# When GpSimd issues its steps of weight sums in a one-core decoder layer

## The chip, the core and the metric

The kernel runs on one core of a Trainium2 chip. The core has TensorE (matrix products, into PSUM), VectorE, ScalarE, GpSimd and SyncE, each with a queue of its own that it works through in order, and sixteen DMA engines that serve the queues of DMAs that SyncE, ScalarE and GpSimd issue. The metric is the device time of one launch in microseconds; lower is better. A time stands for the median of several runs.

## The reference

One layer of a hybrid decoder on 2048 tokens of width 1024, all in float32:

```python
h = rmsnorm(x, mix_norm_g)
q, k, v, g, u = split(h @ w_in)                     # 4 x 512 columns and 512 for the pooling
y_ret  = silu(g) * head_rmsnorm(retention(q, k, v, positions), ret_gn_g)
y_pool = pool_mixer(u, pool_w, pool_scale)
x = x + concat([y_ret, y_pool]) @ w_out
x = x + cross_attn(rmsnorm(x, xa_norm_g), mem_n, wq, wkv, wo)     # 4 heads, 256 memory tokens
a = rmsnorm(x, ffn_norm_g) @ w_up                   # 2 * 2816 columns
c = causal depthwise convolution of width 3 along the tokens, plus a bias
x = x + (silu(c_gate) * c_val) @ w_down
return rmsnorm(x, final_norm_g)
```

Retention and the rotary embedding use `positions`; the cross-attention is a softmax over the 256 memory tokens.

## The kernel before

**Precision and products.** A float32 product is made of three passes of TensorE in a reduced format: each operand is split into a high and a low part (`split`, lines 230 to 237: ScalarE makes the high part, VectorE the low one), and `passes` (lines 239 to 243) issues high x high, high x low, low x high. A `unit` (line 287) multiplies 128 output columns by 1024 tokens: two weight halves times two token halves, so four quarters of twelve passes.

**Stages.** The tokens are worked on in two blocks of 1024 (`for b in range(NB)`, from line 1547 on). Ahead of them stands `folded_weights`, which multiplies weights of the attention and of the pooling with one another; part of it (`wqT`, `wo`, `wout_p`) is spread over the projections of the first block. A block then has:

- its input projections: values, four heads (gate, q, k: three units each, with the retention of the head before spread over them) and four pooling groups, 16 units in all;
- its output projection: 8 units, with the residual `xT` loaded into temporaries `T` ahead of time, the result stored to `Xd` by a DMA that ScalarE issues (L816);
- its attention (`attention`, line 824): for two pairs of heads, eight tiles of tokens each, 16 iterations. The folded weights `Md` are loaded and split ahead (`load_m`, L837); an iteration makes scores on TensorE, softmax on VectorE and ScalarE (L875 to L884), and two iterations later the transposes L852. The norm's statistics (L317 on TensorE, then small steps on VectorE) are taken at the first iteration;
- beside the first block's attention, the rotary tables of the second block (`rope_tables`, line 548), which load `pos` (L555) into a temporary and run on VectorE;
- the attention's output units with `VWd`, and in the first block the loads of the second block's `xT`.

After both blocks comes the gated MLP, which uses a seven-product scheme (Strassen's kind) for its matrix products. It needs sums of weight blocks, and these are what GpSimd makes.

**The steps of weight sums.** `weight_sums` (lines 907 to 941) has 34 jobs: 22 for `w_up` and 12 for `w_dn`. A job has four stages, eight DMAs from DRAM to DRAM: four plain copies (L921), then two, one and one DMAs that add to what is there (L918). A step starts one job and advances those under way by one stage, so that most steps issue eight DMAs of 192 or 256 KB, and there are 37 steps. A step is paced by a tiny ScalarE copy (L936), which `keep_in_program_order` pins behind the ScalarE instruction traced just ahead of it; a GpSimd copy (L937) waits for it, and the step's DMAs are queued behind that on GpSimd. The sums are needed when the MLP starts.

**When a step is taken.** `under[0]` is the generator. Every call of `next(under[0])` is a tick: the first takes a step, and then `spacing[0]` ticks pass until the next:

```python
for _ in range(spacing[0]):
    yield
```

Ticks come from the quarters of `unit` (L301; in the first block's projections, while `slow[0]` is true, from every other quarter) and from the iterations of `attention` (L889; in the first block from i = 5 on). The spacing is 4 at first, 8 in the first block's output projection, 2 in the attentions, 4 afterwards. During the attention's output units the generator is set aside (`paused`).

**The order of work.** The engines' queues are put in order ahead of the run by a scheduler that plans with its own model of times (only the MLP's end is ordered by hand). Each queue is then worked off as planned. SyncE issues nearly all loads, in order, each when its buffer is free: five places `R` for weights, ten temporaries `T`.

Of the kernel before, what the change touches and what calls it, by code (L numbers as in the profile page):

```python
# [119 lines left out]
def trunk(ctx, tc, xT, memT, pos, w_qkgu, w_v, wkv, wqT, wo, wout_r, wout_p, poolT, w_up, w_dn, vecs, consts, outT):  # L120
# [17 lines left out]
    def new_z(dtype):  # L138
        return Arena(cp.tile([P, 8 * T + 4 * EDGE], dtype, tag="Z", name=nm("Z")), 0, 8, T)
# [58 lines left out]
    def mmps():  # L198
        return mmp.tile([P, SUB], F32, tag="mm", name=nm("mm"))
# [6 lines left out]
    def aux():  # L206
        if both[0] and next(turns_) % 3 == 2:
            return single()
        return auxp.tile([P, SUB], F32, tag="aux", name=nm("aux"))

    def small(n=4):
        t = smp.tile([P, 8], F32, tag="sm", name=nm("sm"))
        return t[:, :n]

    def tt(eng, out, a, b, op):
        return eng.tensor_tensor(out=out, in0=a, in1=b, op=op)  # L216

    def ts(eng, out, a, s1, op0, s2=None, op1=None):
        if op1 is None:
            eng.tensor_scalar(out=out, in0=a, scalar1=s1, scalar2=None, op0=op0)  # L220
        else:
            eng.tensor_scalar(out=out, in0=a, scalar1=s1, scalar2=s2, op0=op0, op1=op1)
# [7 lines left out]
    def split(src, hi, lo, g=None):  # L230

        if g is None:
            act.activation(hi, src, AF.Copy)  # L233
            tt(dve, lo, src, hi.bitcast(F32), ALU.subtract)
        else:
            act.activation(hi, src, AF.Identity, scale=g)
            stt(lo, src, g, hi.bitcast(F32), ALU.mult, ALU.subtract)

    def passes(ps, lhs, rhs, start, stop, more=False):
        (lh, ll), (rh, rl) = lhs, rhs  # L240
        pe.matmul(ps, lh, rh, start=start, stop=False, skip_group_check=more)  # L241
        pe.matmul(ps, lh, rl, start=False, stop=False, skip_group_check=more)  # L242
        latest[0] = pe.matmul(ps, ll, rh, start=False, stop=stop, skip_group_check=more)  # L243

    def new_raw():
        r = raws.take()
        r.free()
        return r.f
# [6 lines left out]
    def pairs(raw):  # L255

        out = []
        for h in range(2):
            r = raw[h] if isinstance(raw, list) else raw[:, h * SUB : (h + 1) * SUB]
            pr = new_pair()  # L260
            split(r, pr[:, 0], pr[:, 1])
            out.append(pr)
        return out
# [14 lines left out]
    quarter, slow, spacing = [0], [True], [4]  # L278
# [8 lines left out]
    def unit(raw, rhs, evac, order=range(4)):  # L287


        hs = raw if isinstance(raw, list) else pairs(raw)  # L290
        ps = [mmps() for _ in range(NS)]
        for h in range(2):
            for s in range(NS):
                for j, kk in enumerate(order):
                    k = 4 * h + kk
                    w = [hs[h][:, i, kk * P : (kk + 1) * P] for i in range(2)]
                    passes(ps[s], w, rhs(k, s), h + j == 0, h == 1 and j == 3)
                next(behind[0], None)
                quarter[0] += 1
                if not slow[0] or quarter[0] % 2:  # L300
                    next(under[0], None)  # L301
                if h == 1:
                    evac(s, ps[s])
# [520 lines left out]
    def attention(sums, beside, pace):  # L824


        scl, nscl = (smp.tile([P, 8], F32, tag="scl", name=nm("scl"), bufs=2) for _ in range(2))
        room = B.take(2 * KT)
        third = [Region(B, room.first + KT * i, KT) for i in range(2)] + [new_z(F32R).take(KT)]
        prob = [third[1], third[0]]  # L830

        def load_m(hp):

            out = mw[hp]
            for kp in range(KT // 2):
                raw = new_raw()
                fetched[0] = sp.dma_start(raw.rearrange("p (k n) -> p k n", k=2), Md[hp, 2 * kp : 2 * kp + 2].rearrange("k p n -> p k n"))  # L837
                if hp == 0 and kp == 0:

                    out += [(pr[:, 0], pr[:, 1]) for pr in pairs(raw)]  # L840
                    yield
                    continue
                for i in range(2):
                    u = third[2 * hp].r[:, (2 * kp + i) * T : (2 * kp + i + 1) * T]
                    split(raw[:, i * SUB : (i + 1) * SUB], u[:, :SUB], u[:, SUB:])
                    out.append((u[:, :SUB], u[:, SUB:]))
                yield

        def turn(pt, t, e):
            tp = aux()  # L850
            for j in range(4):
                pe.transpose(tp[:, j * P : (j + 1) * P], e.f[:, j * P : (j + 1) * P], ident)  # L852
            pt4 = pt.r.rearrange("p (i k t) -> p i k t", i=2, t=T)[:, :, :, t * P : (t + 1) * P]
            turned.append(act.activation(pt4[:, 0], tp.rearrange("p (k t) -> p k t", k=4), AF.Copy))
            tt(dve, pt4[:, 1], tp.rearrange("p (k t) -> p k t", k=4), pt4[:, 0].bitcast(F32), ALU.subtract)
            e.free()

        turned.clear()
        mw = [[], []]
        for _ in load_m(0):  # L860
            pass
        more_m = load_m(1)
        late = []
        for i in range(2 * KT):
            hp, t = divmod(i, KT)
            ps = mmps()
            for k in range(KT):
                x2 = [X[:, 2 * k + j, t * P : (t + 1) * P] for j in range(2)]
                passes(ps, x2, mw[hp][k], k == 0, k == KT - 1)
            if i == 0:  # L870
                rn, _, _ = norm_tables(sums, wide=False)
                ts(dve, scl, rn, 1.0 / 16.0, ALU.mult)
                ts(dve, nscl, rn, -1.0 / 16.0, ALU.mult)
            mx, sm = small(2), small(2)
            dve.reduce_max(out=mx, in_=ps.rearrange("p (h m) -> p h m", h=2), axis=AX.X)  # L875
            ts(dve, mx, mx, nscl[:, t : t + 1], ALU.mult)
            e = TT.take()
            for j in range(2):
                act.activation(e.f[:, j * NMEM : (j + 1) * NMEM], ps[:, j * NMEM : (j + 1) * NMEM], AF.Exp,
                               bias=mx[:, j : j + 1], scale=scl[:, t : t + 1], accum_out=sm[:, j : j + 1])  # L880
            dve.reciprocal(sm, sm)
            for j in range(2):
                ej = e.f[:, j * NMEM : (j + 1) * NMEM]
                ts(dve, ej, ej, sm[:, j : j + 1], ALU.mult)  # L884
            if len(late) == 2:
                turn(*late.pop(0))
            late.append((prob[hp], t, e))
            if pace > 1 or i > 4:
                next(under[0], None)  # L889
            if i < KT - 2:  # L890
                next(more_m, None)
            else:
                for _ in range(pace):
                    next(beside, None)

        def end():
            for one in late:
                yield turn(*one)

        return prob, end()  # L900
# [142 lines left out]
    class Up(Member):  # L1043
# [15 lines left out]
        def evac(self, i, ps):  # L1059
            if i == 0:  # L1060
                self.gate = self.place()
            elif i == 1:
                self.val = self.place()
            which, q, how = ((0, 0, 0), (1, 1, 0), (0, 1, 0), (0, 0, 1), (1, 1, 1), (0, 1, 1), (1, 0, 0))[i]
            d = body(self.val if which else self.gate)[:, q * SUB : (q + 1) * SUB]
            if how:
                tt(dve, d, d, ps, ALU.add)
            else:
                act.activation(d, ps, AF.Copy)
            if i > 4:  # L1070
                pending.extend(self.conv(i - 5))
# [396 lines left out]
    def norm_tables(s_acc, wide=True, late=False):  # L1468

        rn = rows_norm(s_acc)  # L1470
        rb, last = [], None
        if wide:
            rb = [TT.take() for _ in range(NS)]
            last = spread(rn, [r.f[:, :SUB] for r in rb], late=late)
        return rn, rb, last
# [71 lines left out]
    for b in range(NB):  # L1547
# [29 lines left out]
        for r in rb:  # L1577
            r.free()
        mix += [pooled[g] for g in range(4)]
        slow[0], spacing[0] = False, (8, 4)[b]  # L1580

        xs = [TT.take() for _ in range(NS)]
        ahead = fetch_x(b, 0)
# [15 lines left out]
        beside = tables() if b + 1 < NB else first_tiles(own)  # L1599
        spacing[0] = (2, 2)[b]  # L1600
        prob, behind[0] = attention(xs, beside, b + 1)
        spacing[0] = 4
        for _ in beside:
            pass
        under, paused = [iter(())], under
# [14 lines left out]
        for n in range(KT):  # L1620
# [3 lines left out]
            def rhs(k, s):  # L1624
                at = (k % 4) * T + s * SUB
                return tuple(prob[k // 4].r[:, i * 4 * T + at : i * 4 * T + at + SUB] for i in range(2))
# [159 lines left out]
```

## Time and profile before

| | |
|---|---|
| median of 3 runs | 2476.74 us (2476.66 to 2477.2) |
| the profiled execution's own time | 2477.48 us |
| its span, first to last instruction | 2475.5 us |
| TensorE busy | 2434.9 us (98%) |
| VectorE, ScalarE busy | 1707.9 us (69%), 1223.2 us (49%) |
| GpSimd busy | 272.1 us (11%) |
| mean granted TensorE clock | 0.994 |
| bytes that the steps' queue (q0) moved | 69.22 MB, 12.4% of the sixteen DMA engines' span |

The page is read from the busy shares to the chain of work that ended last and from there to the waits: idle time of an engine matters only where that engine sets the end. Below, a row of the timeline has the start and the length in us, then engine, line, operation, what it writes and reads and, in brackets, how long its engine stood idle ahead of it and what ended that. A row of the waits has who waited for whom, the total in us, the number of times, the longest. A row of the windows has its stretch and length, then busy time and count for TensorE, its weight loads, VectorE, ScalarE and GpSimd, then the granted clock, the DMA engines' busy share and GB/s. A row of a DMA queue has its packets, MB, and the time that its packets took as a share of all engines; a row of DMA issues has the size of each and the median time from issue to landing.

### The profile page before, as it was taken

What the parts mean: (1) busy time and instruction counts of PE and PEld (TensorE: products, weight loads), DVE (VectorE), ACT (ScalarE), POOL (GpSimd) and SP (SyncE); (2) the same over time, 40 slices, a digit from 0 to 9 for tenths busy, and PEclk for the clock granted to TensorE, in tenths of its full rate; (3) what the DMA queues carried; (4) which work ended last, traced back from release to release, by engine and by line L of the source; (5) the groups of instructions that cost most, each with busy time, mean ns of one, the idle gap of its engine ahead of it and who ended that gap; (6) DMA issues with size and microseconds to landing.
All of it is one profiled execution on the core that took longest, in us unless ns stands there. A gap on an engine that the chain in (4) does not pass through costs nothing.

```text
span 2475.5 us, 33058 instructions
## 1 busy us (share of the span) xinstructions
PE 2434.9 (98%) x11390; PEld 2036.2 (82%) x11390; DVE 1707.9 (69%) x2913; ACT 1223.2 (49%) x2207; POOL 272.1 (11%) x413
## 2 busy tenths in 40 slices
PE   6999999999999999999999999999999999999997
PEld 6888888888888888888888888888888888888886
DVE  8645666565635675574678776897667688867876
ACT  6333423353421223434655565665555677666663
POOL 1001022131113430000000010020000000000000
PEclk8999999999999999999999999999999999999998
DMA  8145677767636767356468665665546468768951
GB/s 287 65 136 159 203 177 196 222 141 246 183 101 154 189 165 205 111 196 246 145 200 283 204 189 158 220 215 174 160 155 217 135 225 301 247 189 276 348 173 68
DMA packets 248216, 474.27 MB, mean 192 GB/s; under 512 B 26864, under 2 KB 54128, under 8 KB 248048
## 3 DMA queue, kind: packets, MB, share of 16 engines
q1 hardware_dynamic: 193328, 374.62, 46.4%
q0 software_dynamic: 30208, 69.22, 12.4%
q10 hardware_dynamic: 24512, 28.32, 3.3%
q8 instruction: 89, 1.46, 0.2%
q14 instruction: 79, 0.65, 0.1%
HBM read 370.87 MB, written 170.39 MB: 219 GB/s over the span
## 4 chain that ended last, share of the span: by engine, by line
PE 96%; DVE 1%; DMA 1%; ACT 1%; issue 0%; POOLq 0%; POOL 0%; SPq 0%; DVEq 0%; ACTq 0%
PE mm L241 30%; PE mm L243 30%; PE mm L242 30%; PE aux L764 1%; PE aux L751 1%; PE aux L852 1%; PE aux L740 1%; PE aux L766 1%; PE aux L317 1%; DMA R<-wo 1%; PE aux L241 1%; PE aux L243 1%; PE aux L242 1%; DVE Z L216 0%; DVE Q L216 0%
## 5 line engine op out<-in xcount | busy, mean ns | idle before, releaser
L241 PE MATMUL mm<-G,Q 128*128 128x512 f32 (+1 forms) x1888 | 727.0, 386 | 17.1 <-ACT Q L233 10.9
L243 PE MATMUL mm<-G,Q 128*128 128x512 f32 (+1 forms) x1888 | 725.7, 385 | 5.8 <-DVE Q L216 5.6
L242 PE MATMUL mm<-G,Q 128*128 128x512 f32 (+1 forms) x1888 | 724.8, 384 | 0.0
L241 PE MATMUL mm<-G 128*128 128x512 f32 (+1 forms) x1380 | 529.0, 385 | 3.1 <-ACT T L474 3.0
L242 PE MATMUL mm<-G 128*128 128x512 f32 (+1 forms) x1380 | 530.8, 385 | 0.0
L243 PE MATMUL mm<-G 128*128 128x512 f32 (+1 forms) x1380 | 528.8, 385 | 0.0
L241 PEld LDWEIGHTS mm<-G,Q 128*128 128x128 f32 x1888 | 358.1, 190 | 86.0 <-ACT Q L233 11.5
L243 PEld LDWEIGHTS mm<-G,Q 128*128 128x128 f32 x1888 | 357.6, 190 | 75.4 <-DVE Q L216 7.1
L242 PEld LDWEIGHTS mm<-G,Q 128*128 128x128 f32 x1888 | 358.1, 190 | 67.9 <-DVE G L216 0.4
L241 PEld LDWEIGHTS mm<-G 128*128 128x128 f32 x1380 | 260.0, 188 | 54.8 <-ACT T L474 3.2
L242 PEld LDWEIGHTS mm<-G 128*128 128x128 f32 x1380 | 260.0, 188 | 51.5
L243 PEld LDWEIGHTS mm<-G 128*128 128x128 f32 x1380 | 259.9, 188 | 51.4
L1023 ACT ACTIVATE G<-R 128x512 fp32r<-128x512 f32 (+1 forms) x272 | 167.0, 615 | 251.2 <-PE mm L242 244.2
L216 DVE TENSOR_TENSOR Z<-Z,mm 128x512 f32<-128x512 f32 x284 | 193.8, 683 | 102.2 <-PE mm L243 102.0
L216 DVE TENSOR_TENSOR Q<-R,Q 128x512 fp32r<-128x512 f32 x235 | 162.6, 695 | 147.2 <-ACT Q L233 133.0
L225 DVE SCALAR_TENSOR_TENSOR Z<-Z,vecs 128x1024 f32<-128x1024 f32 x176 | 224.8, 1281 | 49.9 <-ACT Z L1086 46.4
L216 DVE TENSOR_TENSOR G<-R,G 128x512 fp32r<-128x512 f32 (+1 forms) x268 | 178.4, 675 | 107.7 <-ACT G L1023 75.0
L233 ACT ACTIVATE Q<-R 128x512 fp32r<-128x512 f32 x150 | 93.7, 629 | 259.9 <-PE mm L242 220.0
L1023 ACT ACTIVATE Q<-R 128x512 fp32r<-128x512 f32 (+1 forms) x204 | 125.5, 615 | 96.0 <-PE mm L242 80.4
L216 DVE TENSOR_TENSOR G<-T,G 128x512 fp32r<-128x512 f32 (+1 forms) x201 | 133.2, 677 | 44.2 <-ACT G L972 29.1
L216 DVE TENSOR_TENSOR T<-T 128x512 f32<-128x512 f32 (+3 forms) x218 | 149.5, 690 | 19.3 <-ACT T L357 11.2
L1086 ACT ACTIVATE Z<-Z,vecs 128x1024 f32<-128x1024 f32 x88 | 109.2, 1242 | 34.0 <-DVE Z L216 33.1
(216 smaller groups left out, 2623.2 us busy)
## 6 DMA issues: line engine op xcount, KB each, us to landing
R<-Ud SPq DMA_DIRECT2D x176, 256.0 KB, 2.8
T<-Gd SPq DMA_DIRECT2D x168, 256.0 KB, 4.4
Ud<-w_up POOLq DMA_DIRECT2D x132, 256.0 KB, 8.9
R<-w_up SPq DMA_DIRECT2D x132, 256.0 KB, 3.3
Gd<-Z SPq DMA_DIRECT2D x110, 256.0 KB, 2.8
R<-w_qkgu SPq DMA_DIRECT2D x32, 512.0 KB, 4.4
R<-Dd SPq DMA_DIRECT2D x64, 256.0 KB, 4.2
Gd<-T SPq DMA_DIRECT2D x56, 256.0 KB, 3.5
```

Source lines behind the costliest of these rows:

```text
L216: return eng.tensor_tensor(out=out, in0=a, in1=b, op=op)
L225: dve.scalar_tensor_tensor(out=out, in0=a, scalar=s, in1=b, op0=op0, op1=op1)
L233: act.activation(hi, src, AF.Copy)
L241: pe.matmul(ps, lh, rh, start=start, stop=False, skip_group_check=more)
L242: pe.matmul(ps, lh, rl, start=False, stop=False, skip_group_check=more)
L243: latest[0] = pe.matmul(ps, ll, rh, start=False, stop=stop, skip_group_check=more)
L317: pe.matmul(ps[:, t : t + 1], ap, one, start=True, stop=more is None)
L740: pe.matmul(col(sc, c), self.ch(k, c), self.ch(q, c), start=True, stop=True)
L751: pe.matmul(col(self.kv, c), col(self.kn.f, c), self.ch(v, c, h * T), start=True, stop=True)
L764: pe.matmul(col(y, c), col(self.pr.f, c), self.ch(v, c, h * T), start=True, stop=self.cur[c] is None)
L1023: act.activation(p2[:, 0, :w], self.raw[i].f[:, :w], AF.Copy)
L1086: act.activation(self.c[g].f, a[:, 2:], AF.Identity, bias=cb[:, f : f + 1], scale=cw[2][:, f : f + 1])
```

## The change

Four values change. In the first block's projections no tick comes any more (before: every other quarter). In its attention the ticks start at i = 2, not at i = 5. The spacing in its output projection is 4 instead of 8, and in the second block's projections 3 instead of 4.

```diff
@@ -297,7 +297,7 @@
                     passes(ps[s], w, rhs(k, s), h + j == 0, h == 1 and j == 3)
                 next(behind[0], None)
                 quarter[0] += 1
-                if not slow[0] or quarter[0] % 2:
+                if not slow[0]:
                     next(under[0], None)
                 if h == 1:
                     evac(s, ps[s])
@@ -885,7 +885,7 @@
             if len(late) == 2:
                 turn(*late.pop(0))
             late.append((prob[hp], t, e))
-            if pace > 1 or i > 4:
+            if pace > 1 or i > 1:
                 next(under[0], None)
             if i < KT - 2:
                 next(more_m, None)
@@ -1577,7 +1577,7 @@
         for r in rb:
             r.free()
         mix += [pooled[g] for g in range(4)]
-        slow[0], spacing[0] = False, (8, 4)[b]
+        slow[0], spacing[0] = False, (4, 4)[b]
 
         xs = [TT.take() for _ in range(NS)]
         ahead = fetch_x(b, 0)
@@ -1599,7 +1599,7 @@
         beside = tables() if b + 1 < NB else first_tiles(own)
         spacing[0] = (2, 2)[b]
         prob, behind[0] = attention(xs, beside, b + 1)
-        spacing[0] = 4
+        spacing[0] = 3
         for _ in beside:
             pass
         under, paused = [iter(())], under
```

## The prediction

> **What bounds the kernel now.** I read the page first: the span, the busy shares, the chain of work that ended last.
>
> ```profile
> span 2475.5 us, 33058 instructions
> PE 2434.9 (98%) x11390; PEld 2036.2 (82%) x11390; DVE 1707.9 (69%) x2913; ACT 1223.2 (49%) x2207; POOL 272.1 (11%) x413
> PE 96%; DVE 1%; DMA 1%; ACT 1%; issue 0%; POOLq 0%; POOL 0%; SPq 0%; DVEq 0%; ACTq 0%
> ```
>
> TensorE is the bound. GpSimd's steps are not on the chain, so moving them gains only where their transfers now make TensorE wait, and costs only where they will make it wait. So I next read the waits of TensorE from 60 to 960 us, the stretch in which all steps run.
>
> ```profile
> PE mm L241 <- ACT T L474: 3.0, 1, 3.0
> PE mm L241 <- ACT G L233: 0.9, 1, 0.9
> PE mm L241 <- ACT T L492: 0.3, 1, 0.3
> ```
>
> That is everything: 4.2 us. The one of 3.0 us lies in the first block's projections, among the steps that the change takes away. The timeline around it, and the issues of two loads of `wo` (us from issue to landing stand last; the first load was issued at 191.1 us, the second at 205.2 us):
>
> ```profile
> 200.87 0.19 POOL L937 COPY halo<-halo 128x2 f32<-128x2 f32 x1 [55.39 <-ACT halo L936]
> 203.02 3.03 POOL L921 DMA_DIRECT2D Ud<-w_up  x4
> 212.59 1.15 ACT L233 ACTIVATE G<-R 128x512 fp32r<-128x512 f32 x2 [8.14 <-DMA R<-wo]
> 220.79 1.15 ACT L233 ACTIVATE G<-R 128x512 fp32r<-128x512 f32 x2 [5.81 <-DMA R<-wo]
> 222.37 0.82 ACT L474 ACTIVATE T<-mm,vecs 128x256 f32<-128x256 f32 x2
> 223.24 0.58 PE L241 MATMUL mm<-G 128*128 128x256 f32 x1 [2.99 <-ACT T L474]
> ...
> R<-wo SPq DMA_DIRECT2D x1, 512.0 KB, 3.7
> R<-wo SPq DMA_DIRECT2D x1, 512.0 KB, 7.4
> ```
>
> The third step starts at 200.87 us and GpSimd is still issuing its DMAs at 206. The `wo` load of 205.2 us goes out into them and takes 7.4 us, not 3.7. ScalarE stands still for it (8.14 us), issues the next split, stands still again for the next load (5.81 us), and only then empties the PSUM bank (L474) that TensorE needs. The stall has a second price, in the granted clock (the number ahead of the last two of a row; TensorE's busy time is the second):
>
> ```profile
> 220.30:223.20 2.90, 0.00 (x0) 0.00 (x0) 0.95 (x3) 2.41 (x6) 0.00 (x0) 0.97 0.00 0
> 223.20:227.20 4.00, 3.96 (x21) 3.96 (x22) 2.99 (x5) 3.50 (x9) 0.00 (x0) 0.59 0.41 136
> 930.00:936.00 6.00, 5.14 (x21) 3.60 (x20) 3.90 (x6) 2.32 (x5) 2.67 (x4) 1.00 1.06 288
> ```
>
> After 2.99 us of idleness the clock is 0.59 for 4.0 us: 0.41 x 4.0 = **1.6 us** more. The 0.9 us stall at 931 us left it at 1.00.
>
> **The change part by part.** 34 jobs with four stages each make 37 steps. By the counts of calls (a step, then as many empty calls as the spacing says) they lie before: 8 in the first block's projections, 4 in its output projection, 6 in its attention, 16 in the second block's projections, 3 in its output projection; after: 0, 8, 7, 22, 0.
>
> *Each step's own instructions.* These move and are not added: one ScalarE copy, one GpSimd copy, eight DMAs.
>
> ```profile
> L936 ACT ACTIVATE halo<-consts x37: 187/189/221, 80.0 to 937.0; 128x2 f32<-128x2 f32 x37
> 385.04 0.72 POOL L937 COPY halo<-halo 128x2 f32<-128x2 f32 x1 [19.17 <-ACT halo L936]
> 387.86 3.38 POOL L921 DMA_DIRECT2D Ud<-w_up  x4
> 450.38 0.55 POOL L937 COPY halo<-halo 128x2 f32<-128x2 f32 x1 [15.76 <-ACT halo L936]
> 514.16 0.46 POOL L937 COPY halo<-halo 128x2 f32<-128x2 f32 x1 [57.71 <-ACT halo L936]
> ```
>
> ScalarE: 4 + 1 + 6 more copies of 0.19 us in three stages, under its idle time (49% busy). GpSimd: a step holds it from 385.04 to 391.2 us, and in these stages it has nothing behind the steps that anything waits for. Both I cost at nothing. The cost is in the DMA engines.
>
> *First block's projections.* Without the third step the load of 205.2 us lands 7.4 - 3.7 = 3.7 us earlier, all behind it on ScalarE moves up by as much, and L474 ends before TensorE is ready (it waits 2.99 us). Gain 2.99 + 1.6 = **4.6 us**. What is late next: the 0.3 us at L492, far from any step; I leave it. Bounds of the gain: 0 (if that load stays slow) to 5.8 (with the 0.9 and 0.3 us waits gone too).
>
> *First output projection, 8 steps for 4.* Shares of the sixteen DMA engines by queue from 385 to 483 us (q0 carries the steps, q1 SyncE's loads, q10 ScalarE's stores):
>
> ```profile
> q0 software_dynamic: 3584, 8.39, 37.8%
> q1 hardware_dynamic: 5575, 11.09, 35.1%
> q10 hardware_dynamic: 2173, 3.96, 11.0%
> ```
>
> Four steps took 0.378 x 98 = 37 us of all engines, 9.3 us each; loads and stores took 45 us. Eight steps take 74: together 119 us in a stretch of 98. So the steps run late by about 20 us and are still moving data from 483 to 500 us, where before there were none between 465 and 514. Inside the output projection I see no stall: TensorE never waits from 380 to 660 us though four steps already lie there, and `xT`, the weights and `Md` are fetched at least a unit (11 us) ahead. Its end and the start of attention are another matter.
>
> *Start of the first attention.* The timeline (ScalarE twice, VectorE twice, TensorE):
>
> ```profile
> 481.06 0.63 ACT L233 ACTIVATE Z<-R 128x512 fp32r<-128x512 f32 x1 [0.88 <-DMA R<-Md]
> 481.07 0.33 ACTq L816 DMA_DIRECT2D Xd<-T  x1
> ...
> 489.35 0.49 DVE L220 TENSOR_SCALAR T<-T,consts 128x512 f32<-128x512 int32 x1 [5.13 <-DMA T<-pos]
> 496.77 0.62 DVE L220 TENSOR_SCALAR T<-T,sm 128x256 f32<-128x256 f32 x2
> ...
> 498.78 0.60 PE L852 MATMUL aux<-consts,T 128*128 128x128 f32 x4
> ```
>
> A serial chain: ScalarE waits for the third `Md` load and then issues the store of `Xd`; its landing (485.8 us) frees the temporary into which SyncE loads the positions; VectorE waits for those (5.13 us) with the first multiplication of the rotary table, and the statistics of the norm are queued behind it; so are the first softmax and its last scaling, which ends at 497.39. TensorE's transposes L852 start at 498.78. **The whole chain has 1.4 us of slack.** Its transfers now, in order Md, Xd, pos, with q1 in 469 to 489 us; then like loads beside steps (674 to 693 us: q1, `w_qkgu`, `rope_d`; at 408 to 412 us: Xd):
>
> ```profile
> q1 hardware_dynamic: 1696, 4.46, 64.1%
> R<-Md SPq DMA_DIRECT2D x3, 512.0 KB, 4.8
> Xd<-T ACTq DMA_DIRECT2D x1, 256.0 KB, 4.7
> T<-pos SPq DMA_DIRECT2D x2, 128.0 KB, 2.9
> ...
> q1 hardware_dynamic: 1009, 3.15, 42.1%
> R<-w_qkgu SPq DMA_DIRECT2D x5, 512.0 KB, 9.5
> T<-rope_d SPq DMA_DIRECT2D x2, 256.0 KB, 8.8
> Xd<-T ACTq DMA_DIRECT2D x4, 256.0 KB, 8.7
> ```
>
> No row shows this chain beside steps, so I bound it. Lowest: no delay. Highest: each link as slow as its like, 4.7 + 4.0 + 5.9 = 14.6 us. Between: q1 moves 4.46 MB here in 20 us; beside steps it moved 3.15 MB in 19 us, 0.166 MB/us, at which 4.46 MB take 26.9 us, and the positions come last. I take that, **6.9 us**, since it is the row of the same queue with as many large loads in a line. TensorE then waits 6.9 - 1.4 = 5.5 us, and 1.6 us for the clock as at 223 us: **7.1 us**.
>
> [...]
>
> *Rest of attention, second block's projections.* 7 steps for 6 start with i = 2, every 11 us: 65 us of engine time where little else moves; the end is no later than before. In the second block, 22 steps of 9.3 us, 205 us in some 260, beside one 512 KB load of `w_qkgu` per unit, fetched units ahead; and by the pinning to ScalarE's preceding instruction (L936), those of ticks 4 to 10 gather behind the first pool evacuation, away from the `rope_d` loads. Cost 0. The second output projection loses three steps: it has one wait of 0.9 us, on a split that no DMA feeds; gain 0.
>
> Sum: -4.6 + 7.1 = +2.5 us. The profiled execution took 2477.48 us (span 2475.5), the median of the runs is 2476.74; 2476.74 + 2.5 = **2479.2 us**.
>
> **The rivals.**
> (a) Attention's start doesn't stall: the steps are done by then, or VectorE's order puts the norm's statistics ahead of the positions. For it: the order is made anew for each program. Against: in this one VectorE stood 5.13 us before the positions, so the planner already takes that load for earlier than it is. Time: 2476.74 - 4.6 = 2472.1; with every wait gone, 2470.9.
> (b) Slower: the three links add up in full. For it: they are serial by wait, not only by bandwidth, and q10's stores compete too. 14.6 - 1.4 + 1.6 - 4.6 = +10.2: 2486.9. A delay above 4.4 us loses more than the projections gain; above 9.4 us the loss passes 0.2%.
> (c) The `wo` stall stays (another order on ScalarE, another load in the way) and the attention's comes on top: +7.1, 2483.8. Against: only that step's DMAs lay across that load.
>
> **How the numbers follow.** Chances: forecast 0.45, (a) 0.30, (b) 0.17, (c) 0.08. About 0.2% (5 us) is what a measurement of this kernel can tell from no change: below 2471.8 is faster, above 2481.7 slower. Faster takes a third of (a): 0.10. Slower takes (b), (c) and a sixth of the forecast: 0.32. The rest, 0.58, is within. Range 2471.6 to 2486.0: it cuts the ends of (a) and (b). The forecast's own: 2476 to 2483.
>
> **What would show it.** Right: no wait at L474 near 220 us and a clock of 1.00 from 213 to 240; q0 busy from 385 to about 590 without a pause; a wait of TensorE of some 5 us before L852 near 494 to 500 us, VectorE waiting for `T<-pos` about 12 us, and a clock below 1 after it; no step behind the second block's projections. Wrong: a wait for `wo` in the projections, no wait at L852, or new waits of TensorE in the output projection or in the second block (loads late that I called covered).

## The result and the profile after

The changed kernel takes **2485.94 us** (median of six runs, 2485.05 to 2486.32) against 2477.55 for the kernel before on the same chip (six runs, 2476.66 to 2478.64). The ratio is 1.0033 with a 95% interval of 1.0020 to 1.0046: **8.4 us slower**. The profiled execution has a span of 2484.1 us. Of the eleven runs of one kernel below (spacing 3 alone) one took 4285.6 us at a granted clock of 0.57; its median is that of the other ten. From the page of after, in the order in which the page of before was read:

```profile
span 2484.1 us, 33049 instructions
...
PE 2438.0 (98%) x11390; PEld 2037.7 (82%) x11390; DVE 1708.1 (69%) x2913; ACT 1223.8 (49%) x2207; POOL 269.4 (11%) x413
...
PE 92%; DMA 3%; DVE 3%; ACT 1%; issue 1%; POOLq 0%; SPq 0%; POOL 0%; ACTq 0%; DVEq 0%
```

The work is the same: TensorE has 11390 matrix instructions in both. Its share of the chain fell from 96% to 92%, and VectorE's and the DMAs' rose to 3% each, so the loss shows as waits; TensorE's own busy time grew by 3.1 us, which fits the slower clock behind them. The next view is again that of TensorE's waits (who waited for whom, total, number, longest), for after from 60 to 1250 us (behind that the waits are the same four in both kernels):

```profile
PE aux L317 <- DVE T L216: 3.4, 1, 3.4
PE mm L243 <- DVE Q L216: 3.0, 1, 3.0
PE aux L751 <- ACT T L746: 1.0, 1, 1.0
PE mm L241 <- ACT G L233: 0.9, 1, 0.9
PE mm L241 <- ACT T L474: 0.8, 1, 0.8
PE mm L242 <- DVE Q L216: 0.7, 1, 0.7
PE aux L852 <- DVE T L220: 0.6, 1, 0.6
```

The wait at L474 shrank from 3.0 to 0.8 us. Two of 3 us are new, and VectorE is named in both. To place them I follow the same instructions through both kernels. The view of one source line has the count, the shortest, median and longest duration in ns, and the first and last start; the landmark is the first start. Before, then after:

```profile
L317 PE MATMUL aux<-consts,Z x16: 206/250/352, 62.0 to 63.9; 128*128 128x1 f32 x16
...
L740 PE MATMUL aux<-Z x8: 275/275/275, 348.1 to 348.9; 128*128 128x128 f32 x8
...
L317 PE MATMUL aux<-consts,T x16: 164/250/250, 482.8 to 487.6; 128*128 128x1 f32 x16
...
L317 PE MATMUL aux<-consts,T x32: 164/250/250, 666.0 to 678.6; 128*128 128x1 f32 x32
```

```profile
L317 PE MATMUL aux<-consts,Z x16: 167/250/250, 61.2 to 62.8; 128*128 128x1 f32 x16
...
L740 PE MATMUL aux<-Z x8: 275/275/275, 343.8 to 344.5; 128*128 128x128 f32 x8
...
L317 PE MATMUL aux<-consts,T x16: 164/250/271, 483.6 to 493.2; 128*128 128x1 f32 x16
...
L317 PE MATMUL aux<-consts,T x32: 164/250/250, 672.8 to 685.3; 128*128 128x1 f32 x32
```

The differences are -0.8, -4.3, +0.8 and +6.8 us. So the first block's projections gained 3.5 us, the output projection lost 5.1, the first attention with its output units lost 6.0, and 1.8 us came after that. Of these, 1.1 us lie in the last part of the run: from the end of the wait at L319 to that of the wait at L1269 before takes 5.05 us and after 6.15, with the clock at half from 2.3 us ahead of that end in before and from 5.8 us ahead in after (2462.2 of 2464.5 and 2467.3 of 2473.0 us). No edit reaches that place, and the traces of the other kernels have 5.04 to 6.40 us there, so I take it for the scatter of single executions. So, in part at least, are the 0.8 us by which this one was ahead at its start (granted clock from 28 to 63 us: 0.80 in before, 0.85 in after). The remaining 0.7 us I leave open.

**The first loss, at 408 us.** The DMA queues and issues of the stretch from 392.5 to 402 us, first before, then after:

```profile
q0 software_dynamic: 471, 1.31, 46.6%
...
T<-xT SPq DMA_DIRECT2D x5, 256.0 KB, 3.3
```

```profile
q0 software_dynamic: 519, 1.31, 60.0%
...
T<-xT SPq DMA_DIRECT2D x6, 256.0 KB, 9.1
```

The residual's loads go out into two steps in a row (GpSimd's copies at 391.57 and 399.96 us) and take 9.1 us instead of 3.3. What follows in after, in order of time:

```profile
405.79 0.69 DVE L216 TENSOR_TENSOR T<-T,mm 128x512 f32<-128x512 f32 x1 [1.74 <-DMA T<-xT]
...
409.70 0.69 DVE L216 TENSOR_TENSOR T<-T,mm 128x512 f32<-128x512 f32 x1 [3.22 <-DMA T<-xT]
410.30 0.68 DVE L216 TENSOR_TENSOR Q<-R,Q 128x512 fp32r<-128x512 f32 x1
...
411.04 0.50 PE L243 MATMUL mm<-G,Q 128*128 128x512 f32 x1 [2.96 <-DVE Q L216]
```

VectorE stands for the residual. TensorE does not need the residual; it needs the low part of the next weights (Q), which is queued behind it. Before, the same three additions ran without a wait for a load:

```profile
407.76 1.97 DVE L216 TENSOR_TENSOR T<-T,mm 128x512 f32<-128x512 f32 x3 [2.90 <-PE mm L243]
```

**The second loss, at the attention's start.** Step eight is late: GpSimd takes it up at 462.62 us, must wait with its adding DMAs for those of earlier stages, and issues its last DMA after 472.88. The three last `Md` loads take 9.3 us (before: 4.8). They also go out 4.2 us later than in before (477.17 against 472.97): the `Md` load ahead of them, issued just before step eight, landed at 471.31 us instead of 467.12, and the splits that set the places in `R` free, its own and those behind it on ScalarE, moved by as much.

```profile
462.62 0.20 POOL L937 COPY halo<-halo 128x2 f32<-128x2 f32 x1
...
465.96 0.85 POOL L918 DMA_DIRECT2D Ud<-Ud  x1 [3.13 <-DMA Ud<-Ud]
...
472.88 2.41 POOL L921 DMA_DIRECT2D Ud<-w_up  x4
...
486.18 1.15 ACT L233 ACTIVATE Z<-R 128x512 fp32r<-128x512 f32 x2 [5.49 <-DMA R<-Md]
...
489.00 0.63 ACT L233 ACTIVATE Z<-R 128x512 fp32r<-128x512 f32 x1 [0.17 <-DMA R<-Md]
...
490.57 0.61 ACT L357 ACTIVATE T<-T 128x512 f32<-128x512 f32 x1
...
491.67 0.68 DVE L216 TENSOR_TENSOR T<-T 128x512 f32<-128x512 f32 x1
492.40 1.05 PE L317 MATMUL aux<-consts,T 128*128 128x1 f32 x8 [3.35 <-DVE T L216]
...
498.01 0.49 DVE L220 TENSOR_SCALAR T<-T,consts 128x512 f32<-128x512 int32 x1 [5.66 <-DMA T<-pos]
```

ScalarE splits `Md` as it lands; the squares of the last residual (L357) are queued behind, and the statistics L317 need them. The positions come after that, at 498 us, and cost 0.6 us more at L852. Both losses have a second price in the clock (windows; the number ahead of the last two is the granted clock):

```profile
408.00:411.00 3.00, 0.08 (x1) 0.00 (x0) 1.30 (x3) 0.58 (x2) 0.00 (x0) 1.00 1.09 285
411.00:414.00 3.00, 2.96 (x10) 2.35 (x11) 3.00 (x6) 2.24 (x5) 0.00 (x0) 0.74 1.05 385
414.00:417.00 3.00, 3.00 (x11) 2.41 (x10) 1.80 (x3) 0.00 (x0) 0.00 (x0) 0.69 1.03 378
...
494.50:498.50 4.00, 4.00 (x12) 3.09 (x12) 0.49 (x2) 0.00 (x0) 0.00 (x0) 0.59 0.45 149
```

Worked out from these windows, that is 0.26 x 3 + 0.31 x 3 = 1.7 us after the first and 0.41 x 4 = 1.6 us after the second. With the waits that makes 3.0 + 1.7 + 0.7 (L242, at 478 us) = 5.4 us against the 5.1 of the landmarks, and 3.4 + 0.6 + 1.6 = 5.6 against 6.0.

### The profile page after: what moved, and what is told of

The parts are those of the page before. It is cut to its first block, busy times and chain, and to the rows that moved or that the text cites. A ratio compares the mean times of both kernels' runs of the same rounds, so it can differ in the third digit from the quotient of the medians.

```text
span 2484.1 us, 33049 instructions
## 1 busy us (share of the span) xinstructions
PE 2438.0 (98%) x11390; PEld 2037.7 (82%) x11390; DVE 1708.1 (69%) x2913; ACT 1223.8 (49%) x2207; POOL 269.4 (11%) x413
## 4 chain that ended last, share of the span: by engine, by line
PE 92%; DMA 3%; DVE 3%; ACT 1%; issue 1%; POOLq 0%; SPq 0%; POOL 0%; ACTq 0%; DVEq 0%
PE mm L243 29%; PE mm L241 29%; PE mm L242 29%; DVE T L216 1%; DMA T<-Xd 1%; DVE Z L216 1%; PE aux L751 1%; PE aux L764 1%; PE aux L740 1%; PE aux L766 1%; PE aux L317 1%; PE aux L243 1%; PE aux L241 1%; PE aux L242 1%; DMA T<-xT 0%
## 5 line engine op out<-in xcount | busy, mean ns | idle before, releaser
L241 PE MATMUL mm<-G,Q 128*128 128x512 f32 (+1 forms) x1888 | 727.5, 386 | 16.1 <-ACT Q L233 10.2
L243 PE MATMUL mm<-G,Q 128*128 128x512 f32 (+1 forms) x1888 | 726.4, 386 | 8.8 <-DVE Q L216 8.7
L242 PE MATMUL mm<-G,Q 128*128 128x512 f32 (+1 forms) x1888 | 725.4, 385 | 0.0
L242 PE MATMUL mm<-G 128*128 128x512 f32 (+1 forms) x1380 | 530.2, 385 | 0.0
L241 PE MATMUL mm<-G 128*128 128x512 f32 (+1 forms) x1380 | 528.4, 385 | 0.8 <-ACT T L474 0.8
L243 PE MATMUL mm<-G 128*128 128x512 f32 (+1 forms) x1380 | 528.2, 385 | 0.0
L241 PEld LDWEIGHTS mm<-G,Q 128*128 128x128 f32 x1888 | 358.5, 190 | 84.8 <-ACT Q L233 10.8
L243 PEld LDWEIGHTS mm<-G,Q 128*128 128x128 f32 x1888 | 358.1, 190 | 78.7 <-DVE Q L216 10.4
L242 PEld LDWEIGHTS mm<-G,Q 128*128 128x128 f32 x1888 | 358.4, 190 | 67.9 <-DVE G L216 0.4
L241 PEld LDWEIGHTS mm<-G 128*128 128x128 f32 x1380 | 259.4, 188 | 52.3 <-ACT T L474 1.0
L242 PEld LDWEIGHTS mm<-G 128*128 128x128 f32 x1380 | 259.5, 188 | 51.4
L243 PEld LDWEIGHTS mm<-G 128*128 128x128 f32 x1380 | 259.3, 188 | 51.5
```

## The experiments

The theory after the result: the bytes of the steps hold back loads that are needed soon; engines that work in order pass that to TensorE; its idleness can halve the clock (0.50 from 412.5 to 415.8 us, behind the wait of 2.96 us). The rivals: the steps' instructions or the planner's new order make the stalls; the early ticks of the attention make the second one; density as such does harm. All ratios are to the kernel before, timed on the same chip (medians there 2476.8 to 2477.5 us), with a 95% interval.

| kernel | median us | ratio |
|---|---|---|
| before, no ticks in the first projections | 2478.65 | 1.0008 (1.0000 to 1.0017) |
| before, output projection at spacing 4 | 2490.99 | 1.0061 (1.0048 to 1.0075) |
| before, attention's ticks from i = 2 | 2477.44 | 1.0003 (0.9995 to 1.0012) |
| before, second block at spacing 3 | 2476.68 | 0.9998 (0.9988 to 1.0007) |
| after, output projection back at spacing 8 | 2472.68 | 0.9983 (0.9974 to 0.9991) |
| after, an eighth of the bytes there | 2472.76 | 0.9984 (0.9975 to 0.9993) |
| after, steps only in units 0 to 3 there | 2477.43 | 1.0001 (0.9992 to 1.0009) |
| after, steps only in units 4 to 7 there | 2473.57 | 0.9985 (0.9976 to 0.9993) |
| after, no steps there, spacing 2 in the second block | 2472.32 | 0.9980 (0.9971 to 0.9989) |
| after, xT two units ahead | 2482.88 | 1.0020 (1.0011 to 1.0029) |
| after, without the last step there | 2479.25 | 1.0005 (0.9996 to 1.0014) |
| after, the last two together | 2478.19 | 1.0002 (0.9993 to 1.0011) |

### One value at a time

**No ticks in the first block's projections**, on the kernel before.

```diff
-                if not slow[0] or quarter[0] % 2:
+                if not slow[0]:
```

> The kernel before with one value changed: no ticks in the first block's projections. Theory (the transfers of the steps hold back the loads beside them): the 3.0 us wait at L474 and its half clock go, nothing else changes, -3.5 us as in the changed kernel up to 343 us (4.6 at most): 2473 to 2474. The output projection still has 4 steps and no wait; the steps left over go to the second block, beside loads fetched units ahead, and cost nothing there. Rival (moving a step only moves its price): a wait of some 3 us turns up where the left-over steps now run, 2477 or more.

Measured: 2478.65, no gain; the rival is right. The projections did gain: the wait at L474 is gone, and at 1007.9 us (the second attention's first L317, before at 1012.8) the kernel is 4.9 us ahead. All of it is lost at the start of that attention, where the left-over steps now lie (eight in the output projection ahead, the last at 1002 us, and three behind, at 1028 to 1045 us). The waits, the one load concerned and two rows of the timeline:

```profile
PE aux L852 <- DVE T L220: 3.6, 2, 3.5
```

```profile
R<-Md SPq DMA_DIRECT2D x3, 512.0 KB, 13.0
```

```profile
1011.31 1.15 ACT L233 ACTIVATE Z<-R 128x512 fp32r<-128x512 f32 x2 [4.79 <-DMA R<-Md]
...
1027.55 1.12 PE L852 MATMUL aux<-consts,T 128*128 128x128 f32 x4 [3.49 <-DVE T L220]
```

It is the second loss of the changed kernel over again, half a millisecond later. But the same run holds a counterexample. Its second output projection has a step in every unit, as the changed kernel's first has; from 930 to 1000 us the residual's loads are as slow as there (first row), VectorE stands for one of them (second row), and yet no wait of TensorE lies in that stretch (the usual 0.9 us comes ahead of it, at 926 us):

```profile
T<-xT SPq DMA_DIRECT2D x13, 256.0 KB, 10.1
```

```profile
941.50 0.69 DVE L216 TENSOR_TENSOR T<-T,mm 128x512 f32<-128x512 f32 x1 [3.64 <-DMA T<-xT]
```

A late load is not yet a stall. Here VectorE has made the next low parts (Q) at 936.58 us, ahead of the addition that waits, and makes the ones after it at 943.31 us, early enough; in the changed kernel Q stands behind the addition. What counts is what is queued behind the instruction that waits, and when TensorE needs that.

**Spacing 4 in the first output projection**, on the kernel before.

```diff
-        slow[0], spacing[0] = False, (8, 4)[b]
+        slow[0], spacing[0] = False, (4, 4)[b]
```

> The kernel before with one value changed: spacing 4 instead of 8 in the first output projection. Theory: the steps' transfers alone make both new stalls, +5.1 us in the output projection (VectorE waits for xT) and some +6.3 at the start of the attention (ScalarE waits for Md, VectorE for pos): 2477.5 + 11.4 = 2489, with the L474 wait still there. Rival (the attention's stall comes from its ticks starting at i = 2): only +5, 2482.6.

Measured: 2490.99, 14.2 us slower. The theory holds and is even a little short: this one value makes both losses (a wait of 5.5 us at L243, one of 2.2 us at L317), without any early tick in the attention. Each of the two goes with half clock that lasts twice as long as in the changed kernel (6.7 us against 3.3): 0.50 from 413.9 to 420.6 us and from 492.4 to 499.1 us. Here three jobs are already under way from the first block's projections, so every step is a full one of eight DMAs from the first on, while the first three steps of the changed kernel have four, six and seven; that this is why the losses are larger is not shown by itself.

**Attention's ticks from i = 2**, on the kernel before.

```diff
-            if pace > 1 or i > 4:
+            if pace > 1 or i > 1:
```

> The kernel before with one value changed: ticks of the first attention from i = 2 on. Theory: the first step there comes after the transposes L852 have begun, so the start of the attention has no stall: 0, 2477.5 (within 1.5). Rival (these ticks make the stall at the attention's start): +6, 2483.5.

Measured: 2477.44, no difference. The early ticks make no loss by themselves, and in the changed kernel the first step of the attention comes at 508.94 us, behind both waits, so they have no part in the second loss.

**Spacing 3 in the second block's projections**, on the kernel before.

```diff
-        spacing[0] = 4
+        spacing[0] = 3
```

> The kernel before with one value changed: spacing 3 instead of 4 in the second block's projections, so that the three steps of its output projection are done earlier. Theory (loads there are fetched long before their use; in this kernel no wait hangs on those three steps): 0, 2477.5 within 1.5; the value of this edit lies only in keeping left-over steps out of the start of the second attention once the first block's projections have none. Rival (denser steps cost by themselves, or the last steps of the kernel before cost something that no wait shows): 1.5 us or more either way.

Measured: 2476.68, no difference, as expected. Alone it is worth nothing; what it is worth beside the first edit, the next kernel suggests.

**Spacing 8 put back, the other three kept**, on the changed kernel.

```diff
-        slow[0], spacing[0] = False, (4, 4)[b]
+        slow[0], spacing[0] = False, (8, 4)[b]
```

> The changed kernel with one value put back: spacing 8 in the first output projection, the other three edits kept. Theory: the projections' gain stays (-3.5) and neither new stall is left: 2474, 12 us below the changed kernel. Rival 1 (the early ticks make the attention's stall): 2480. Rival 2 (the denser steps of the second block cost something): between 2475 and 2479, with a wait of TensorE between 660 and 960 us.

Measured: 2472.68, **4.1 us faster than before and 12.5 us faster than the changed kernel**, each taken against the kernel before on its own chip (+8.4 and -4.1). Neither new wait is left, and the `Md` loads of the second attention, which took 13.0 us in the first experiment, take this long:

```profile
R<-Md SPq DMA_DIRECT2D x3, 512.0 KB, 4.2
```

So of the four values one loses 12 to 14 us, one gains 4 us if the steps that it displaces end before the second attention, and one (the early ticks) does nothing alone. That spacing 3 is what ends them in time is argued from the steps: their last one starts at 1045.5 us in the first experiment and at 951.5 us here. This kernel also has the early ticks, which move one step more out of the way, and no run has the first edit with spacing 3 alone.

### Bytes, not instructions

**An eighth of the bytes**, on the changed kernel.

```diff
-                pool.dma_start(d[i], a, max_dma_last_dim=2048)
+                pool.dma_start(d[i][:m], a[:m], max_dma_last_dim=2048)
...
-        live, jobs, at = [], [sums(*j) for j in jobs], 0
+        live, jobs, at = [], [sums(*j, 16 if i < 8 else P) for i, j in enumerate(jobs)], 0
```

> The changed kernel with the same steps at the same places, the same copies on ScalarE and GpSimd and the same number of DMAs, but the DMAs of the first eight jobs (those begun in the first output projection) move 16 rows of 128; the other rows of their plain copies are fetched beside the second block's projections and their additions are left out, so these eight sums are incomplete. Theory (it is the bytes): xT lands in 3 to 5 us, Md in 5, neither new stall is there, and the time is that of the kernel with spacing 8 put back, 2472.7 (2472 to 2475). Rival (it is the steps' instructions, their number of DMAs or the order that the planner made of them): the waits in the output projection and before L317 stay, 2484 to 2486.

Measured: 2472.76, the theory's number to 0.1 us. In the output projection VectorE's order is that of the changed kernel, and the steps stand where they stood, with as many DMAs; the loads are fast again, from 392.5 to 402 us:

```profile
T<-xT SPq DMA_DIRECT2D x6, 256.0 KB, 4.1
```

For the first loss what the DMAs carry is the cause; steps, their instructions and VectorE's order are not. (Bytes and packets fell together, q0 from 519 packets and 1.31 MB to 221 and 0.23 in this stretch, so the two aren't told apart.) At the attention's start the planner has put a few of VectorE's instructions and the L317 themselves in another order, so for the second loss this kernel says the same but less cleanly.

**Steps in the first half or in the second half** of the output projection, on the changed kernel (first half; the second has `n < 4`).

```diff
         for n in range(KT):
+            slow[0] = b == 0 and n >= 4
             raw = new_raw()
```

> The changed kernel with ticks only in the first four of the eight units of the first output projection, at spacing 4. Theory (a stall belongs to the step that lies across the load): the wait of 3.1 us near 408 us and its half clock stay (+5), the attention starts without one, and the steps left over cost at most 1 us: 2472.7 + 5 = 2478. Rival (what counts is the backlog of all steps): both stalls shrink or both stay.

> The changed kernel with ticks only in the last four of the eight units of the first output projection, at spacing 4. Theory: no wait near 408 us; steps lie across the Md loads and the positions as in the changed kernel, so the waits before L317 and L852 stay, +5 to +7: 2472.7 + 6 = 2479. Rival (the backlog of the early steps makes the late Md): no wait before L317, 2473.

Measured: 2477.43 and 2473.57. The first is as the theory has it: the wait at L243 stays (3.5 us), none at L317. (Its profiled execution is the slowest of its eleven, 2481.04.) The second is not: I expected the wait at L317 with four steps near it, and it is 0.3 us, with 0.6 at L852. The rival (backlog) is right so far: these steps start with fresh jobs, the last of them issues its DMAs from 455.6 to 461.8 us, before GpSimd falls behind, and the three `Md` loads take 6.4 us, not 9.3. In the changed kernel the eighth step is queued behind seven others, and its last DMA is issued 2.7 us ahead of those loads (474.5 against 477.2), not 7.9 (461.8 against 469.7).

**Density where loads have time**, on the changed kernel: no step in the first output projection, one every second quarter in the second block.

```diff
-        spacing[0] = 3
+        spacing[0] = 2
```

> The changed kernel with no tick in the first output projection and spacing 2 instead of 3 in the second block's projections, a step every three quarters (some 8.5 us), which the transfers of a step (9.3 us of all engines) more than fill. Theory (what makes a stall is a load used soon after its issue, not the density of the steps): the w_qkgu loads there are fetched units ahead, so no wait of TensorE appears from 660 to 960 us, and the time is 2472.7 within 1.5. Rival (density as such makes stalls): new waits there, 2476 or more.

Measured: 2472.32, the fastest here, though not told apart from the two at 2472.7. (The expectation miscounts: spacing 2 is a step every two quarters, so it asks for even more than it says. The prediction words it the same way, a step and then as many empty calls; the code takes one step in as many calls as the spacing says, and the prediction's counts go by that.) The windows from 660 to 930 us, of before and of this kernel:

```profile
660.00:930.00 270.00, 270.00 (x1367) 229.11 (x1366) 161.80 (x372) 60.09 (x159) 91.68 (x143) 1.00 0.65 162
```

```profile
660.00:930.00 270.00, 268.77 (x1359) 227.48 (x1358) 162.88 (x373) 61.50 (x171) 154.15 (x242) 1.00 1.00 252
```

The DMA engines go from 65% to 100% busy. TensorE's one wait in the second window is the usual one at L241, which before comes at 931 us and so outside the window; here it ends at 926 us and is 1.2 us long instead of 0.9. So density as such cost 0.4 us at most here, where the loads are fetched units ahead.

### Two repairs

**xT two units ahead**, on the changed kernel.

```diff
-        ahead = fetch_x(b, 0)
+        ahead = [fetch_x(b, n) for n in range(2)]
...
-            got, ahead = ahead, fetch_x(b, n + 1) if n + 1 < KT else None
+            got = ahead.pop(0)
+            if n + 2 < KT:
+                ahead.append(fetch_x(b, n + 2))
```

> The changed kernel, all steps kept, but the residual xT of the first output projection (and of the second) is loaded two units ahead instead of one, as far as the ten temporaries allow. Theory (the stall near 408 us comes of xT loads issued 8 to 12 us before VectorE needs them, which take 7 to 12 us beside the steps): that stall and its half clock go, -5; the attention's stall stays, since Md is loaded as before: 2481. Rival (the temporaries don't come free earlier, so the loads move little): 2484 to 2486.

Measured: 2482.88, between the two. It is inconclusive on the cause: one pair of loads moved up, the next six were still issued from 394 to 398 us, because the temporaries are not free before. The wait at L243 fell to 1.8 us and the clock stayed at 1.00, but the next kernel has 1.6 us there without any load moved up, so the fall need not be this repair's; the attention's wait stayed (3.8 us at L317).

**No step in the last unit**, and **both together**.

```diff
         for n in range(KT):
+            slow[0] = b == 0 and n == KT - 1
             raw = new_raw()
```

> The changed kernel without the last of the eight steps of the first output projection (no tick in its last unit; that step's work moves to the attention). Theory A (the last step, whose transfers end at 485 us across the Md loads of 477 to 489, makes the attention's stall): the waits before L317 and L852 go, -6: 2479.5, as with ticks in the first half alone. Theory B (backlog: GpSimd's issues have fallen behind by then, so that step seven takes the place of step eight): waits of 2 to 4 us stay there, 2482 to 2485.

> Both together: xT two units ahead and no step in the last unit of the first output projection. If the two stalls are independent and each has the cause named, neither is left, with seven steps in the output projection: 2473 to 2474. If one repair only moves the traffic into the other place: 2477 or more.

Measured: 2479.25 and 2478.19. The first meets theory A's number, but not for its reason alone. The wait at L317 is gone, yet a new one stands at L852, and the first output projection lost less here (1.6 us at L243), for a reason that I can't name. Two rows of VectorE, and TensorE's waits there:

```profile
491.11 0.49 DVE L220 TENSOR_SCALAR T<-T,consts 128x512 f32<-128x512 int32 x1 [6.92 <-DMA T<-pos]
491.51 0.16 DVE L222 TENSOR_SCALAR sm<-aux 128x8 f32<-128x8 f32 x1
```

```profile
PE aux L852 <- DVE T L220: 2.8, 2, 2.6
```

This is the chain of the prediction, link by link: the positions late, the norm's statistics (sm) queued behind them, the softmax, L852. Its slack can be checked with it. Before, VectorE began on the positions 2.5 us after the second group of L317 (489.35 against 486.9); here 6.9 us after (491.11 against 484.2), 4.4 us later; less the 1.4 us of slack that is 3.0, and the row has 2.8. The two repairs together leave 2.3 us at L243 with its half clock and 0.6 at L852. So the expectation of independent repairs failed too: removing the last step cures L317, but neither repair frees the residual's loads from steps two and three.

## Why the prediction was right and wrong

- **The sign and the places outside the output projection were right, the size was not**: +8.4 us (+8.6 in the traces) against +2.5. The time, 2485.94, lies just inside the stated range, 0.06 us below its upper end, which was drawn near rival (b); as (b) isn't what happened, that is luck. The forecast's own range ended at 2483, and the outcome held likeliest (0.58), a time within some 5 us of before, did not come. The step that failed is one sentence, "Inside the output projection I see no stall", which priced that part at 0. It was worth +5.1 us, nearly all of the gap of 5.9 to 6.1. The reason given was that TensorE never waits there in the profile of before, and that `xT` is fetched at least a unit ahead. But that there is no wait shows only that there is some slack, not how much, and the lead was misread: in before the same two loads, the fourth and the sixth of the six, went out at 400.91 and 402.34 us for additions that began at 407.76 and ran one after the other, so their lead was some 7 us, not 11. In after, the two loads concerned were issued at 396.53 and 397.96 us, 7.5 and 8.5 us before VectorE was free for them (405.79 - 1.74 and 409.70 - 3.22), and took 9.2 and 11.6; before, these six took 2.8 to 4.2. The row of `Xd` beside steps, 8.7 us, which the prediction itself quoted for the attention, uses up such a lead. The question "what is queued behind the waiting instruction" was put for the positions and not for the residual.
- **Gain in the first projections**: 4.6 forecast, 3.5 measured. This miss of 1.1 us and the opposite one at the attention's start cancel, by chance. By the same two landmarks it was 4.4 in the kernel before with this one edit and 4.2 in the changed kernel at spacing 8 (343.3 - 61.6 and 342.9 - 61.0 against 348.1 - 62.0). The mechanism is right (no wait of 3 us, clock 1.00 there), but the 1.6 us for the clock was read from one execution: in the trace of the kernel with spacing 3 alone the same wait, 2.97 us long, left the clock at 1.00 (last section). What is late next was missed: 0.8 us remain at L474, and 1.0 us is new at L751, for ScalarE; that wait stands at 0.7 to 1.0 us in all ten kernels without these ticks.
- **Attention's start**: 7.1 forecast, 6.0 measured, by the forecast's price of a half clock (1.6 us, measured 1.6). The `Md` loads took 4.5 us longer (9.3 us beside a backlogged q0 against 4.8) and went out 4.2 us later, the positions were late as said, and VectorE's order was the one that was read. But the link that TensorE waited for first was another: L317, through ScalarE's squares behind `Md`, one link earlier than the positions. The prediction followed the chain along the DMAs and did not ask who else stands behind `Md` on ScalarE. The kernel without the last step shows the forecast chain alone: it was real, and mostly hidden behind the earlier one.
- **The steps**: 0, 8, 7 and 22 as counted. They were late, but by less than the 20 us of the forecast: the eighth step's last DMA landed at 485.2 us. Then q0 rested until 509, so the row expected of q0, busy without a pause to 590, was not there.
- **Rest of the attention and second block**: 0 forecast. The second block's projections have no wait, and the kernel with spacing 2 shows that even full DMA engines (100% busy from 660 to 930 us) cost 0.4 us at most there. That the displaced steps would lose the gain without spacing 3 was not seen: the prediction gave the three steps that leave the second output projection a gain of 0, which holds for the kernel before (2476.68), not for one whose first projections have none.
- **The rivals**: (b), 2486.9, and (c), 2483.8, lie near in time and neither is what happened. (b) wanted 14.6 us of delay in one place, (c) the `wo` wait to stay. Two losses of 5 to 6 us in two places gave the time.

## What to carry to other kernels

When background transfers are moved, list every load that will lie beside them with three numbers: issue to landing now, the same beside such transfers elsewhere in the trace, and issue to first use; the load whose use comes sooner than the second number makes the stall, if what TensorE needs is queued behind that use (the two `xT` loads of the first loss: 9.2 and 11.6 us beside the steps, 7.5 and 8.5 us to their use). Place bulk traffic where loads have the longest lead, and there as densely as the engines allow (100% busy cost 0.4 us at most here); keep it away from the starts of stages (6.0 us lost at the first attention's). And look where the displaced work ends: a gain in one stage (4.9 us by 1007.9 us, in the kernel without ticks in the first projections) was lost whole at another stage's start until a second value was changed as well.

## What the runs showed of the hardware

What idleness of TensorE does to its clock is shown by three kernels. First the same wait at the same place: the row of TensorE's wait, then a window behind it, of the kernel with xT two units ahead and of the one with both repairs:

```profile
410.30 0.50 PE L243 MATMUL mm<-G,Q 128*128 128x512 f32 x1 [1.83 <-DVE Q L216]
```

```profile
410.20:414.00 3.80, 3.70 (x16) 3.09 (x17) 3.80 (x8) 1.79 (x4) 0.00 (x0) 1.00 1.06 361
```

```profile
409.46 0.50 PE L243 MATMUL mm<-G,Q 128*128 128x512 f32 x1 [2.33 <-DVE Q L216]
```

```profile
411.00:414.30 3.30, 3.30 (x9) 2.56 (x8) 3.25 (x6) 1.78 (x3) 0.00 (x0) 0.50 1.00 392
```

After 1.83 us of idleness the clock stays at 1.00; after 2.33 us it is 0.50 from 411.0 to 414.3 us, and 1.00 again from 414.4 us on. The figures between 0.59 and 0.74 above are such stretches cut by a window: the clock is 0.50 from 412.5 to 415.8 and from 494.4 to 497.7 us in the changed kernel, and from 223.1 to 226.4 us in before. A stretch of 3.3 us at 0.50 costs some 1.7 us (0.50 x 3.3) where TensorE is busy.

But the length of the wait doesn't settle it. In the kernel with spacing 3 alone the wait at L474, which before is 2.99 us long and followed by half clock, is as long, and the clock stays:

```profile
223.00 0.39 PE L241 MATMUL mm<-G 128*128 128x256 f32 x1 [2.97 <-ACT T L474]
```

```profile
223.00:227.20 4.20, 4.20 (x30) 3.98 (x31) 3.18 (x6) 3.70 (x9) 0.00 (x0) 1.00 0.43 148
```

So neither does a wait of more than 2.3 us always halve the clock (the one of 2.97 us didn't) nor is a price of 1.6 us sure; the same wait has it in one trace and not in the other. What decides it no run here shows.
